# Up projection of a ConvFFN on fp16 halves with one scale for all its weights, measured by squares in the mLSTM

## The chip, the cores and the metric

The kernel runs on one core of one Trainium2 chip. The core has a matrix engine (TensorE, PE in the profile, with its weight loads as PEld), a vector engine (VectorE, DVE), an activation engine (ScalarE, ACT), a general engine (GpSimd, POOL) and a sequencer that issues most DMAs (SyncE, SP). ACT issues DMAs too, in order with its other instructions. The metric is the device time of one execution in microseconds (us), as a median of several.

## The reference

One layer of a diffusion backbone with D = 1024, 1024 latent tokens and 256 context tokens: a modulated RMSNorm, one input projection that feeds a bidirectional mLSTM with 4 heads and a windowed attention with 16, a gated merge with residual, and then a ConvFFN with 2816 hidden units. Cut to what matters here:

```python
def conv_ffn(h, w_up, conv_w, conv_b, w_down):
    L = h.shape[1]
    u = h @ w_up                       # (1024, 1024) @ (1024, 5632)
    r = CONV_W // 2
    up = jnp.pad(u, ((0, 0), (r, r), (0, 0)))
    acc = conv_b
    for j in range(CONV_W):
        acc = acc + up[:, j:j + L] * conv_w[j]
    a, g = jnp.split(acc, 2, axis=-1)
    return (jax.nn.silu(g) * a) @ w_down

x_mid = x + g1[:, None, :] * y         # y: the merged branches, mLSTM and attention
x = x_mid + g2[:, None, :] * conv_ffn(modulate(rms_norm(x_mid, norm2_w[l]), sh2, sc2), ...)
```

Inputs and outputs are fp32.

## The kernel before

The program is one stream of code in stages: modulation and input projections, attention, mLSTM, branch projections and merge, up projection with convolution and gate, down projection. The framework places each instruction in its engine's order by a schedule of its own; each engine then runs its instructions strictly in that order, and waits on semaphores. So a row's place on an engine is not its place in the code.

**Pairs.** Products that need more accuracy than one pass gives are made from a high and a low half of each operand: `split_from` (L50) writes the high half by an ACT copy (`copy_act`, L46, its instruction is L47) and the low half by a DVE subtraction (L54, or L56 with a scale). Three matmuls make one product: high by high, low by high, high by low (`mm3`, L158, L163 to L165 in the trace; `product`, L2011, L2015 to L2017). The input and mLSTM projections use fp16 halves, with scales measured from the weights themselves (`ScaledWeights`, squares on L112). The branch, up and down projections use fp32 halves of a rounded kind (fp32r), where no scale is needed.

**The up projection** (`Units`, L2020) treats w_up in 22 units of 1024 x 256 columns, each read by one 1 MB DMA. A unit is multiplied by a scheme of 7 products instead of 8, with sums of quarters of the weights (`prep`, `prep2`: tiles s, then q1, q2, r1, r2 as pairs) and of the activations (`put`, L1872: b11, b21, b22, t1 to t4 as pairs, made once). Each product has 4 steps of 3 matmuls of 128x128 by 128x512, into PSUM tiles pa, pb, pc. ACT and DVE take these out into ua and ug; `conv_gate` (L2145) makes convolution and gate of them on ACT and DVE (tile cv), and `hidden_sums` makes sums for the down projection. The loop at L2227 runs one unit after another, the splits of the next unit beside the products of this one. The pools op4 (10 tiles of 128x1024 fp32) and op2 (4 of 128x512) hold pair halves.

**The mLSTM** runs head by head (loop L1569). For head h+1 it prepares the two weight groups (`prepare`, squares wjw on L112), splits them (whkv and wlkv for keys and values, whqo and wlqo for queries and the output gate), then multiplies the latent blocks one by one (`proj_kv`, L1308: 8 blocks of 128 tokens, 24 matmuls each; k and VH are ACT copies, VL a DVE split), transposes the keys (`trans_k`, kT to kh and kl), updates states (`states`, dC and C, with CH an ACT copy), and projects the queries (`proj_q`, q to qh and ql). `core` (L1446) multiplies S from queries and keys, masks and decays it (ub), splits it (sh, sl) and makes the outputs (o, i, nm). `proj_o` and the tiles mo and sg are the output gate. In between, `branch_sums` (L1530) loads pieces of the branch weights and of the attention output on ACT's queue (s_ba, t_at, s_bm), forms sums for the branch projections on DVE and stores them; its tile has two buffers, so that a load waits for the store of the second-last set.

Of the kernel before, what the change touches and what calls it, by code (L numbers as in the profile page):

```python
# [171 lines left out]
@with_exitstack  # L172
def layer_kernel(ctx: ExitStack, tc: tile.TileContext, A: dict, out: bass.AP, dbg=None):
    nc = tc.nc
    dbg = dbg or {}

    cp = ctx.enter_context(tc.tile_pool(name="cp", bufs=1, reuse_waits="tile"))
    dr = ctx.enter_context(tc.tile_pool(name="dr", bufs=1, space=DRAM, reuse_waits="tile"))

    ident = cp.tile([P, P], F32, name="ident")  # L180
    nc.sync.dma_start(ident, A["ident"])
    expo = cp.tile([P, 16], F32, name="expo")
    nc.gpsimd.memset(expo, -0.5)
# [71 lines left out]
    if dbg.get("stop") in ("hT", "att"):
        ph1.close()
        psx_t.close()
        psx.close()
        return
    with ExitStack() as st:  # L260
        stage_mlstm(E, st)
    if "mlT" in dbg:
        dump(nc, tc, mlT_d, dbg["mlT"])
    E.gcx.close()
    ph1.close()
    if dbg.get("stop") == "ml":
        psx_t.close()
        psx.close()
        return
    with ExitStack() as st:  # L270
        stage_tail(E, st)
    psx_t.close()
    psx.close()
# [977 lines left out]
def stage_mlstm(E, st):  # L1251
# [56 lines left out]
    def proj_kv(h):  # L1308
        w, f = H[h].pop("wkv"), H[h]["fkv"]
        ks, vs = [None] * NBLK, [None] * NBLK  # L1310
        for j in orders(h)[0][1]:
# [10 lines left out]
            else:  # L1322
# [207 lines left out]
    def branch_sums():  # L1530
# [21 lines left out]
        for j, o in enumerate(res):  # L1552
            nc.sync.dma_start(E.sums_d[n][:, j, i], o)

    rwp = st.enter_context(tc.tile_pool(name="mlr4", bufs=4, reuse_waits="tile"))
    prepare(0)
    bp = st.enter_context(tc.tile_pool(name="mlb", bufs=15, reuse_waits="tile"))
# [3 lines left out]
    proj_q(0)  # L1561
    proj_kv(0)
    E.kvx.close()
    trans_k(0)
    states(0)
    masked(0)
    decays(0, nullcontext())
    for _ in range(2):
        branch_sums()  # L1569
    for h in range(MLH):  # L1570
        core(h)
        proj_o(h)
# [12 lines left out]
        if h + 1 < MLH:  # L1585
            proj_q(h + 1)
            for _ in range((3, 4, 3)[h]):
                branch_sums()


def stage_tail(E, st):
# [46 lines left out]
    def x512(name, dt=F32R, pool=None):  # L1638
# [2 lines left out]
            nx[0] += 1  # L1641
        return xts[pool].tile([P, 512], dt, tag="x", name=name)


    g1b = tp1.tile([P, D], F32, name="g1b")
    g2b = tp1.tile([P, D], F32, name="g2b")
# [174 lines left out]
        nc.sync.dma_start(g1b, E.g_d[0].to_broadcast([P, D]))  # L1821
    branch("m", sgm_d, 6)

    def norm_factors():

        nc.vector.scalar_tensor_tensor(m2[:, 1], m2[:, 1], 1.0, vecT[:, V_N2 : V_N2 + KT], op0=ALU.add, op1=ALU.mult)
        nc.vector.tensor_scalar(m2[:, 1], m2[:, 1], float(D) ** 0.5, None, op0=ALU.mult)

    sM.close()

    accp = sA.enter_context(tc.tile_pool(name="accp", bufs=8, side="right", reuse_waits="tile"))
# [93 lines left out]
    def weight_sums(k, a0, a1, b0, b1, eng=None):  # L1925
# [8 lines left out]

    psc = E.psx_s
    U = Units(
        nc, lambda j: A["w_up"][j], lambda n: rawp.tile([P, KT, 256], F32, tag="raw", name=n), op4, op2,
        lambda tag, n: dict(A=mm_tile, F=E.fl_tile, B=tp_tile, C=lambda n: E.c_tile(n))[tag](n),
        lambda tag, n: accp.tile([P, L], F32, tag="a", name=n), B,
    )  # L1940
# [3 lines left out]
    for i, b in enumerate((4, 5, 6, 7, 0, 1, 2, 3)):  # L1944
# [7 lines left out]
    norm_factors()  # L1952
# [16 lines left out]
    square(5)  # L1969
    scale(4)  # L1970
    U.lead(0)
    U.prep_apart(0, lambda n, dt=F32R: x512(n, dt, 1))
    scale(5)
    first_half(H)
    project(1, 6, w)
# [44 lines left out]
class Units:  # L2020

    def __init__(self, nc, src, raw, op4, op2, bank, out, B):
        self.nc, self.src, self.raw, self.op4, self.op2, self.bank, self.out, self.B = nc, src, raw, op4, op2, bank, out, B
        self.raws, self.R1, self.mid, self.S, self.Q = {}, {}, {}, {}, {}

    @staticmethod
# [5 lines left out]
        return pair[o : o + 4]  # L2034

    def pair(self, j, nm, new, src):
        p = self.v(new(f"{nm}h{j}")), self.v(new(f"{nm}l{j}"))
        split_from(self.nc, *p, src)
        return [(p[0][:, k], p[1][:, k]) for k in range(p[0].shape[1])]

    def lead(self, j):
        self.raws[j] = raw = self.raw(f"ur{j}")
        self.nc.sync.dma_start(raw, self.src(j))
        if j != 2:
            self.R1[j] = self.pair(j, "r1", self.op4, raw[:, :, 0:P])

    def lead_first(self, j):

        raw = self.v(self.op4(f"uf{j}", F32))
        self.nc.sync.dma_start(raw, self.src(j)[:, :, 0:P])  # L2050
        self.R1[j] = self.pair(j, "r1", self.op4, raw)

    def first_mm(self, j):
        nc, B, r1 = self.nc, self.B, self.R1.pop(j)
# [17 lines left out]
    def prep(self, j):  # L2072
# [3 lines left out]
        t(s12[:, 0:4], a21, a22, op=ALU.add)  # L2076
        t(s12[:, 4:8], s12[:, 0:4], a11, op=ALU.subtract)
        self.S[j] = s12
        self.Q[j] = [self.pair(j, "q1", self.op4, s12)]

    def prep2(self, j):
        raw, t = self.raws.pop(j), self.nc.vector.tensor_tensor
# [4 lines left out]
        self.Q[j] += [self.pair(j, "q2", self.op4, s34), self.pair(j, "r2", self.op2, a22)]  # L2087

    def prep_apart(self, j, new):
# [3 lines left out]
        s1, s2, s3, s4 = [self.v(new(f"s{i}_{j}", F32)) for i in range(1, 5)]  # L2093
# [4 lines left out]
        self.Q[j] = [sum([self.pair(j, f"q1{i}", new, s) for i, s in enumerate((s1, s2))], [])]  # L2098
        self.S[j] = s3, s4

    def prep2_apart(self, j):
        h, lo = [self.v(self.op4(f"q2{x}{j}")) for x in "hl"]
        for i, s in enumerate(self.S.pop(j)):
            split_from(self.nc, h[:, 4 * i : 4 * i + 4], lo[:, 4 * i : 4 * i + 4], s)
        r2 = self.pair(j, "r2", self.op2, self.raws.pop(j)[:, 4:8, P:256])
        self.Q[j] += [[(h[:, k], lo[:, k]) for k in range(8)], r2]

    def rest(self, j):
# [328 lines left out]
```

## Time and profile before

| | us |
|---|---|
| median of 3 runs (1849.45 to 1855.98) | 1850.99 |
| the profiled execution | 1858.65 |
| its span in the trace | 1856.9 |
| mean granted clock of TensorE, share of full speed | 0.987 |
| DVE idle until ACT's copy q2h was there (L54), 21 units | 15.8 |
| ACT busy in the window 690 to 975 us (the mLSTM) | 149.44 |

The page gives busy time and its share of the span for each engine, then the chain of work that ended last, and groups of instructions with their mean duration and the idle time ahead of them. A matmul's duration overlaps the next matmul's; the pace of TensorE is read from the distance between two starts. A row of the timeline gives start and duration in us, engine, line, operation, written and read tiles, the form, how many such rows were merged, and in brackets how long the engine idled ahead of it and what ended that.

### The profile page before, as it was taken

Reading aid. Unit: us, or ns where it says so; the run is one execution under the profiler, and the core shown is the slowest. Engines: PE = TensorE matmul, PEld = TensorE weight load, DVE = VectorE, ACT = ScalarE, POOL = GpSimd, SP = SyncE. Lnnn points to the kernel's source line nnn. Section 1 sums busy time; section 2 is a strip of 40 time slices with the busy share of each in tenths; the row PEclk is TensorE's granted clock in tenths of the full one; section 3 lists DMA queues with packets and bytes.
Section 4 is the critical chain, followed back from the end, with each engine's and each line's share of the span. In section 5 each row is a group of like instructions: output and inputs, shape, how many; then the busy total and the mean of one; then the engine's idle time right before and its main releaser. Section 6 shows DMA issues by size and latency. Waiting matters only on the chain.

```text
span 1856.9 us, 27874 instructions
## 1 busy us (share of the span) xinstructions
PE 1795.2 (97%) x9207; PEld 1286.0 (69%) x9207; DVE 1418.6 (76%) x2864; ACT 1070.7 (58%) x2229; POOL 510.5 (27%) x747
## 2 busy tenths in 40 slices
PE   7889999999998899989999999999999999999999
PEld 3855555555555565656668887878888888888887
DVE  3848878888788685858687787698988998896665
ACT  4747777878787564646356563375444444464441
POOL 2467769687762630303020021000000000000000
PEclk9899999999999899999999999999999999999999
DMA  8647988888787724260449936413454544599751
GB/s 336 234 138 147 195 174 177 190 179 196 148 181 138 217 94 161 79 210 32 148 160 359 362 101 221 168 57 125 159 211 180 186 172 154 197 321 369 262 171 68
DMA packets 302193, 342.47 MB, mean 184 GB/s; under 512 B 176208, under 2 KB 200672, under 8 KB 299232
## 3 DMA queue, kind: packets, MB, share of 16 engines
q1 hardware_dynamic: 287648, 314.47, 56.1%
q10 hardware_dynamic: 14400, 26.22, 4.3%
q8 instruction: 72, 1.18, 0.3%
q14 instruction: 73, 0.60, 0.1%
HBM read 224.61 MB, written 76.16 MB: 162 GB/s over the span
## 4 chain that ended last, share of the span: by engine, by line
PE 77%; DVE 7%; DMA 5%; ACT 5%; issue 4%; POOL 3%; ACTq 0%; SPq 0%; POOLq 0%; DVEq 0%
PE g L706 8%; PE pq L706 6%; PE pa L2015 4%; PE pa L2017 4%; PE pa L2016 4%; PE po L706 3%; PE dx L2015 2%; PE dx L2017 2%; PE dx L2016 2%; PE pb L2017 2%; PE pb L2016 2%; PE pb L2015 2%; PE yb L2015 2%; PE yb L2016 2%; PE yb L2017 2%
## 5 line engine op out<-in xcount | busy, mean ns | idle before, releaser
L850 DVE CUSTOM_DVE_ANT_0 s<-s,maskA,nsink 128x640 f32<-128x640 f32 (+1 forms) x128 | 117.5, 918 | 75.0 <-PE s L845 74.6
L866 DVE TENSOR_TENSOR P<-s,P 128x640 f16<-128x640 f32 (+1 forms) x128 | 100.7, 787 | 1.0 <-ACT s L861 1.0
L860 ACT ACTIVATE P<-s,st 128x640 f16<-128x640 f32 (+1 forms) x128 | 98.3, 768 | 4.2
L706 PE MATMUL g<-hH,fh 128*128 128x512 f16 x256 | 97.9, 382 | 0.0
L706 PE MATMUL g<-hH,fl 128*128 128x512 f16 x256 | 97.8, 382 | 0.0
L706 PE MATMUL g<-hL,fh 128*128 128x512 f16 x256 | 97.7, 382 | 0.0
L861 ACT ACTIVATE s<-s,st 128x640 f32<-128x640 f32 (+1 forms) x128 | 93.9, 734 | 0.0
L706 PEld LDWEIGHTS <-hH 128*128 128x128 f16 x640 | 62.1, 98 | 36.5 <-DVE t L770 0.4
L858 ACT ACTIVATE st<-st,shift 128x1 f32<-128x1 f32 x128 | 37.6, 294 | 85.4 <-DVE st L850 84.7
L706 PE MATMUL pq<-wha,hH 128*128 128x384 f16 (+1 forms) x256 | 83.9, 328 | 0.1
L706 PE MATMUL pq<-wha,hL 128*128 128x384 f16 (+1 forms) x256 | 83.9, 328 | 0.0
L706 PE MATMUL pq<-wla,hH 128*128 128x384 f16 (+1 forms) x256 | 83.9, 328 | 0.0
L706 PEld LDWEIGHTS <-fh 128*128 128x128 f16 x512 | 48.1, 99 | 47.9 <-issue 1.6
L2153 ACT ACTIVATE cv<-ua,vecT 128x1024 f32<-128x1024 f32 x22 | 27.4, 1246 | 83.9 <-DVE ua L2126 83.9
L1424 POOL TENSOR_SCALAR kwh<-k,gcall 128x128 fp32r<-128x128 f32 x72 | 33.1, 463 | 154.4 <-PE dC L164 57.1
L163 PE MATMUL kv<-whkv,hH 128*128 128x384 f16 x192 | 63.3, 330 | 6.0 <-DVE VL L56 6.0
L2015 PE MATMUL dx<-dwh,dfh 128*128 128x512 f32 (+1 forms) x176 | 68.3, 388 | 0.0
L2017 PE MATMUL dx<-dwh,dfl 128*128 128x512 f32 (+1 forms) x176 | 68.2, 388 | 0.0
L2016 PE MATMUL dx<-dwl,dfh 128*128 128x512 f32 (+1 forms) x176 | 68.2, 387 | 0.0
L47 ACT ACTIVATE dfh<-drf 128x512 fp32r<-128x512 f32 x55 | 34.3, 628 | 58.5 <-PE dx L2016 26.0
L54 DVE TENSOR_TENSOR dfl<-drf,dfh 128x512 fp32r<-128x512 f32 x55 | 37.7, 691 | 36.5 <-ACT dfh L47 36.4
L164 PE MATMUL kv<-wlkv,hH 128*128 128x384 f16 x192 | 63.2, 329 | 0.4
(691 smaller groups left out, 6253.8 us busy)
## 6 DMA issues: line engine op xcount, KB each, us to landing
ur<-in_w_up SPq DMA_DIRECT2D x22, 1024.0 KB
wmb<-in_w_modB SPq DMA_DIRECT2D x48, 256.0 KB
f_d<-cv SPq DMA_DIRECT2D x22, 512.0 KB
wm<-in_w_modA SPq DMA_DIRECT2D x16, 512.0 KB
fr<-in_w_g SPq DMA_DIRECT2D x32, 256.0 KB
drf<-fs_d SPq DMA_DIRECT2D x15, 512.0 KB
drw<-wt_d SPq DMA_DIRECT2D x14, 512.0 KB
w1b<-in_w_cx SPq DMA_DIRECT2D x16, 388.0 KB
```

Of the source, the lines that this page charges most:

```text
L54: rest = nc.vector.tensor_tensor(lo, src, whole, op=ALU.subtract)
L163: nc.tensor.matmul(ps, lh[:, ls], rh[:, rs], start=start and i == 0, stop=False)
L164: nc.tensor.matmul(ps, lh[:, ls], rl[:, rs], start=False, stop=False)
L706: nc.tensor.matmul(self.ps, x, w, start=self.i == 0, stop=self.i == self.n - 1)
L850: nc.vector.tensor_tensor_reduce(e, e, self.mask, scale=self.ss[:, h : h + 1], scalar=nsink[:, hh : hh + 1], op0=ALU.add, op1=ALU.min, acc ...
L858: nc.scalar.activation(m, st4[:, 8 + h : 9 + h], AF.Identity, bias=shift)
L860: nc.scalar.activation(two[:, :W], e, AF.Exp, bias=m, scale=-1.0)
L861: nc.scalar.activation(e, e, AF.Exp, bias=m, scale=-1.0, accum_out=st4[:, 4 + h : 5 + h])
L866: nc.vector.tensor_tensor(two[:, W : 2 * W], self.e[h], two[:, :W], op=ALU.subtract)
L2015: nc.tensor.matmul(ps, lh, rh, start=start and i == 0, stop=False, skip_group_check=True)
L2016: nc.tensor.matmul(ps, lh, rl, start=False, stop=False, skip_group_check=True)
L2017: nc.tensor.matmul(ps, ll, rh, start=False, stop=stop and i == n - 1, skip_group_check=True)
```

## The change

The up projection's halves become fp16. That needs a scale that brings the weights into fp16's range, one for all of w_up here, in `E.upf[:, 2:3]`. The activations' scale is put into m2, the modulation's factor, and the inverse of both into conv_w, so that the convolution's result stays the same. Both halves of a pair now share one tile of the old size of one half, so that the pools op4, op2 and x512 need half as many slots for pairs.

The scale is measured from the sum of squares of all of w_up: 44 loads of 512 KB on ACT's queue (`up_load`, tile um, a pool of 3 buffers), 44 ACT squares in place with an accumulated sum (`up_square(2)`, after each latent key/value block of heads 1 to 3), and once, in head 3, `up_scales` with one matmul, two small ACT squares, five DVE instructions and ten on POOL. The code of `norm_factors` moves into it. In the trace and in the orders of the changed kernel the lines of the mLSTM lie 5 higher (L1543 for L1538).

```diff
@@ proj_kv
             ks[j] = k
+            if h and j >= NCB:
+                up_square(2)
+            if h == MLH - 1 and vs.count(None) == 1:
+                up_scales()
@@ stage of the mLSTM
+    NUP = 2 * NFC
+    def up_load():
+        n = UP["load"]
+        if n < NUP:
+            raw = UP["raw"][n] = upp.tile([P, 4, 256], F32, tag="up", name=f"um{n}")
+            nc.scalar.dma_start(raw, A["w_up"][n // 2][:, 4 * (n % 2) : 4 * (n % 2) + 4])
+            UP["load"] += 1
+    def up_square(k):
+        for _ in range(k):
+            n = UP["done"]
+            if n < NUP:
+                raw = UP["raw"].pop(n)
+                nc.scalar.activation(raw, raw, AF.Square, accum_out=E.up[:, n : n + 1])
+                UP["done"] += 1
+                up_load()
+    def up_scales():
...
+        nc.tensor.matmul(pb[:, : NUP + 2], E.ones, E.up[:, : NUP + 2], start=True, stop=True)
+        nc.vector.tensor_reduce(f[:, 0:1], pb[:, :NUP], axis=AX.X, op=ALU.add)
...
+        nc.gpsimd.tensor_scalar(f[:, 1:2], f[:, 0:1], 2.0 ** -28, 1e-36, op0=ALU.mult, op1=ALU.add)
+        nc.gpsimd.tensor_tensor(f[:, 2:3], f[:, 1:2], expo[:, 0:1], op=ALU.pow)
...
+        nc.gpsimd.tensor_scalar(m2, m2, f[:, 3:4], None, op0=ALU.mult)
+        cw = vecT[:, V_CW : V_CW + 132]
+        nc.gpsimd.tensor_scalar(cw, cw, f[:, 6:7], None, op0=ALU.mult)
+    upp = ux.enter_context(tc.tile_pool(name="upm", bufs=3, side="right", reuse_waits="tile"))
+    for _ in range(3):
+        up_load()
@@ put
-            B[m][k] = [x512(f"{m}{x}{k}", pool=homes[m]) for x in "hl"]
+            B[m][k] = xpair(f"{m}{k}", homes[m])
@@ Units
     def pair(self, j, nm, new, src):
-        p = self.v(new(f"{nm}h{j}")), self.v(new(f"{nm}l{j}"))
-        split_from(self.nc, *p, src)
+        p = [self.v(t) for t in new(f"{nm}{j}")]
+        split_from(self.nc, *p, src, scale=self.scale)
-        self.Q[j] = [self.pair(j, "q1", self.op4, s12)]
+        self.Q[j] = [self.pair(j, "q1", self.pair4, s12)]
```

The schedule also moves instructions. Three places on ACT matter. The first is the end of head 1's key/value blocks, up to the query copies; whqo are the high halves of the query and gate weights, CH the copies of the state, qh the queries' high half, um the pieces of w_up. Before:

```order
L47 ACTIVATE k_2_8852<-kv_2_8853,wfw_ml_8492 128x128
L47 ACTIVATE VH_2_8879<-kv_2_8853,wfw_ml_8492 128x256
L1546 DMA t_at_0_9051<-attT_d 128x512
L47 ACTIVATE kh_0_8890<-kT_0_8885 128x512
L47 ACTIVATE CH_1_1_8932<-C_1_0_8911 128x258
L47 ACTIVATE kh_1_8899<-kT_1_8894 128x512
L47 ACTIVATE CH_0_1_8945<-C_0_0_8921 128x258
L1546 DMA t_at_0_9051<-attT_d 128x512
L1546 DMA t_at_1_9052<-attT_d 128x512 x2
L47 ACTIVATE qh_0_8990<-q_0_8965,wfw_mlqo_8517 128x512
```

and of the change:

```order
L47 ACTIVATE VH_2_8932<-kv_2_8906,wfw_ml_8503 128x256
L1568 DMA um_8939<-in_w_up 128x1024
L1576 ACTIVATE um_8900,upq<-um_8900 128x1024
L47 ACTIVATE kh_0_8949<-kT_0_8944 128x512
L1568 DMA um_8942<-in_w_up 128x1024
L47 ACTIVATE kh_1_8958<-kT_1_8953 128x512
L47 ACTIVATE CH_1_1_8991<-C_1_0_8970 128x258
L47 ACTIVATE CH_0_1_9004<-C_0_0_8980 128x258
L47 ACTIVATE whqo_0_9008<-wrw_mlqo_0_8511,wfw_mlqo_8528 128x2x384
L47 ACTIVATE whqo_1_9012<-wrw_mlqo_1_8513,wfw_mlqo_8528 128x2x384
L47 ACTIVATE whqo_2_9016<-wrw_mlqo_2_8515,wfw_mlqo_8528 128x2x384
L47 ACTIVATE whqo_3_9020<-wrw_mlqo_3_8517,wfw_mlqo_8528 128x2x384
```

The four whqo splits, which stood ahead of the first key/value block before, now stand behind the last CH, in heads 1 and 2; DVE's wlqo splits follow them there. In head 3 they stay among the blocks.

The second place is ACT at the start of head 2's key/value blocks; wjw are the squares of the next head's weights. Before:

```order
L47 ACTIVATE whqo_3_10159<-wrw_mlqo_3_9704,wfw_mlqo_9715 128x2x384
L47 ACTIVATE k_2_9787<-kv_2_9788,wfw_ml_9690 128x128
L47 ACTIVATE VH_2_9814<-kv_2_9788,wfw_ml_9690 128x256
L1546 DMA t_at_0_10221<-attT_d 128x512 x2
L112 ACTIVATE wjw_ml_0_10894,wqw_ml_10893<-wrw_ml_0_10885 128x768
L47 ACTIVATE k_3_9836<-kv_3_9837,wfw_ml_9690 128x128
L47 ACTIVATE VH_3_9863<-kv_3_9837,wfw_ml_9690 128x256
L1546 DMA t_at_1_10222<-attT_d 128x512 x2
L112 ACTIVATE wjw_ml_1_10896,wqw_ml_10893<-wrw_ml_1_10887 128x768
L112 ACTIVATE wjw_ml_2_10898,wqw_ml_10893<-wrw_ml_2_10889 128x768
```

and of the change:

```order
L1576 ACTIVATE um_9974,upq<-um_9974 128x1024
L1576 ACTIVATE um_9977,upq<-um_9977 128x1024
L1568 DMA um_10016<-in_w_up 128x1024
L47 ACTIVATE k_2_9846<-kv_2_9847,wfw_ml_9749 128x128
L47 ACTIVATE VH_2_9873<-kv_2_9847,wfw_ml_9749 128x256
L1568 DMA um_10068<-in_w_up 128x1024
L1576 ACTIVATE um_10013,upq<-um_10013 128x1024
L47 ACTIVATE k_3_9901<-kv_3_9902,wfw_ml_9749 128x128
L47 ACTIVATE VH_3_9928<-kv_3_9902,wfw_ml_9749 128x256
L1568 DMA um_10071<-in_w_up 128x1024
L1576 ACTIVATE um_10016,upq<-um_10016 128x1024
L1576 ACTIVATE um_10068,upq<-um_10068 128x1024
```

The wjw squares and the branch sums' loads leave the key/value stage for the query stage and `core`, and loads and squares of w_up stand in it.

The third place is ACT between head 3's query copies and its score copies sh. Before:

```order
L47 ACTIVATE qh_0_11400<-q_0_11375,wfw_mlqo_10927 128x512
L47 ACTIVATE qh_1_11429<-q_1_11404,wfw_mlqo_10927 128x512
L47 ACTIVATE sh_1_1_11502<-ub_1_1_10951 128x512
L1475 ACTIVATE nm_1_2_11556<-i_1_2_11552,gcall 128x257
L47 ACTIVATE sh_0_0_11507<-ub_0_0_10954 128x512
```

and of the change:

```order
L47 ACTIVATE qh_0_11557<-q_0_11532,wfw_mlqo_11034 128x512
L1543 DMA s_bm_1_11605<-in_w_bm 128x512
L47 ACTIVATE qh_1_11586<-q_1_11561,wfw_mlqo_11034 128x512
L1543 DMA s_bm_0_11618<-in_w_bm 128x512 x2
L1543 DMA s_bm_1_11619<-in_w_bm 128x512 x2
L47 ACTIVATE sh_1_1_11659<-ub_1_1_11058 128x512
L1480 ACTIVATE nm_1_2_11713<-i_1_2_11709,gcall 128x257
L47 ACTIVATE sh_0_0_11664<-ub_0_0_11061 128x512
```

Four loads of a further branch sum now stand between the query copies and the first score copy.

More of the change, by code (lines that the diff above doesn't have):

```diff
@@ L243, in layer_kernel @@
     E.hs = cp.tile([P, 2], F32, name="hs")
+    E.upf = cp.tile([P, 32], F32, name="upf")
     E.w2 = ScaledWeights(E, tc, ph1)
@@ L1553, in branch_sums @@
             nc.sync.dma_start(E.sums_d[n][:, j, i], o)
+    E.up = mp.tile([P, 64], F32, name="upq")
+    UP = dict(load=0, done=0, raw={})
+    NUP = 2 * NFC
[13 more added lines that the diff above has]
+                up_load()
@@ L1563, in stage_mlstm @@
     E.kvx.close()
+    ux = ExitStack()
+    upp = ux.enter_context(tc.tile_pool(name="upm", bufs=3, side="right", reuse_waits="tile"))
     trans_k(0)
@@ L1588, in stage_mlstm @@
                 branch_sums()
+    ux.close()
 def stage_tail(E, st):
@@ L1642, in x512, with pair16, xpair, pair4 @@
         return xts[pool].tile([P, 512], dt, tag="x", name=name)
+    def pair16(t):
+        n = t.shape[1] // 2
+        return t[:, :n], t[:, n:]
+    def xpair(name, pool):
+        return pair16(xts[pool].tile([P, 1024], F16, tag="x", name=name))
+    def pair4(name):
+        return pair16(op4p.tile([P, 2048], F16, tag="o4", name=name))
+    def pair2(name):
+        return pair16(op2p.tile([P, 1024], F16, tag="o2", name=name))
     g1b = tp1.tile([P, D], F32, name="g1b")
@@ L1936, in stage_tail @@
     U = Units(
-        nc, lambda j: A["w_up"][j], lambda n: rawp.tile([P, KT, 256], F32, tag="raw", name=n), op4, op2,
+        nc, lambda j: A["w_up"][j], lambda n: rawp.tile([P, KT, 256], F32, tag="raw", name=n), op4, pair4, pair2, E.upf[:, 2:3],
         lambda tag, n: dict(A=mm_tile, F=E.fl_tile, B=tp_tile, C=lambda n: E.c_tile(n))[tag](n),
@@ L2020, with __init__ @@
 class Units:
-    def __init__(self, nc, src, raw, op4, op2, bank, out, B):
-        self.nc, self.src, self.raw, self.op4, self.op2, self.bank, self.out, self.B = nc, src, raw, op4, op2, bank, out, B
+    def __init__(self, nc, src, raw, op4, pair4, pair2, scale, bank, out, B):
+        self.nc, self.src, self.raw, self.op4, self.pair4, self.pair2, self.bank, self.out, self.B = nc, src, raw, op4, pair4, pair2, bank, out, B
+        self.scale = scale
         self.raws, self.R1, self.mid, self.S, self.Q = {}, {}, {}, {}, {}
@@ L2044, in lead @@
         if j != 2:
-            self.R1[j] = self.pair(j, "r1", self.op4, raw[:, :, 0:P])
+            self.R1[j] = self.pair(j, "r1", self.pair4, raw[:, :, 0:P])
     def lead_first(self, j):
@@ L2050, in lead_first @@
         self.nc.sync.dma_start(raw, self.src(j)[:, :, 0:P])
-        self.R1[j] = self.pair(j, "r1", self.op4, raw)
+        self.R1[j] = self.pair(j, "r1", self.pair4, raw)
     def first_mm(self, j):
@@ L2086, in prep2, with prep_apart @@
         t(s34[:, 4:8], a12, self.S.pop(j)[:, 4:8], op=ALU.subtract)
-        self.Q[j] += [self.pair(j, "q2", self.op4, s34), self.pair(j, "r2", self.op2, a22)]
-    def prep_apart(self, j, new):
+        self.Q[j] += [self.pair(j, "q2", self.pair4, s34), self.pair(j, "r2", self.pair2, a22)]
+    def prep_apart(self, j, new, new16):
         raw, t = self.raws[j], self.nc.vector.tensor_tensor
         a11, a12, a21, a22 = raw[:, 0:4, 0:P], raw[:, 4:8, 0:P], raw[:, 0:4, P:256], raw[:, 4:8, P:256]
-        s1, s2, s3, s4 = [self.v(new(f"s{i}_{j}", F32)) for i in range(1, 5)]
+        s1, s2, s3, s4 = [self.v(new(f"s{i}_{j}")) for i in range(1, 5)]
         t(s1, a21, a22, op=ALU.add)
@@ L2097, in prep_apart @@
         t(s3, a11, a21, op=ALU.subtract)
-        self.Q[j] = [sum([self.pair(j, f"q1{i}", new, s) for i, s in enumerate((s1, s2))], [])]
+        self.Q[j] = [sum([self.pair(j, f"q1{i}", new16, s) for i, s in enumerate((s1, s2))], [])]
         self.S[j] = s3, s4
     def prep2_apart(self, j):
-        h, lo = [self.v(self.op4(f"q2{x}{j}")) for x in "hl"]
+        h, lo = [self.v(t) for t in self.pair4(f"q2{j}")]
         for i, s in enumerate(self.S.pop(j)):
-            split_from(self.nc, h[:, 4 * i : 4 * i + 4], lo[:, 4 * i : 4 * i + 4], s)
-        r2 = self.pair(j, "r2", self.op2, self.raws.pop(j)[:, 4:8, P:256])
+            split_from(self.nc, h[:, 4 * i : 4 * i + 4], lo[:, 4 * i : 4 * i + 4], s, scale=self.scale)
+        r2 = self.pair(j, "r2", self.pair2, self.raws.pop(j)[:, 4:8, P:256])
         self.Q[j] += [[(h[:, k], lo[:, k]) for k in range(8)], r2]
```

22 lines of the change are left out of this document (17 added, 5 removed).

## The prediction

> **What bounds the kernel now.** I read the busy shares first, then the chain that ended last.
>
> ```profile
> PE 1795.2 (97%) x9207; PEld 1286.0 (69%) x9207; DVE 1418.6 (76%) x2864; ACT 1070.7 (58%) x2229; POOL 510.5 (27%) x747
> PE 77%; DVE 7%; DMA 5%; ACT 5%; issue 4%; POOL 3%; ACTq 0%; SPq 0%; POOLq 0%; DVEq 0%
> ```
>
> TensorE is busy 97% of the span and is 77% of the chain. Those are averages; the change touches two stretches with different limits, the FFN (about 1218 to 1642 us) and the mLSTM (about 690 to 975 us), so I read windows there (columns: length, PE, PEld, DVE, ACT, POOL busy us with counts, PE clock, DMA share, GB/s).
>
> ```profile
> 1300.00:1400.00 100.00, 100.00 (x443) 82.81 (x442) 89.17 (x106) 48.35 (x59) 0.00 (x0) 1.00 0.50 182
> 1225.00:1235.00 10.00, 9.79 (x49) 8.02 (x50) 9.89 (x28) 9.20 (x24) 0.00 (x0) 1.00 0.01 3
> 690.00:975.00 285.00, 270.53 (x1589) 177.05 (x1587) 201.26 (x560) 149.44 (x351) 53.40 (x134) 0.98 0.41 137
> ```
>
> In the FFN's middle PE never rests: a shorter matmul there shortens the kernel, until DVE (89%) takes over. At the FFN's start DVE is already full. In the mLSTM PE rests 14.5 of 285 us and ACT has work for 149; there the change adds work to ACT and the DMA queues.
>
> **What the fp16 operands save.** The row counts 88 `pa<-b11h,r1h` matmuls, 4 for each of 22 units; a unit has 7 products of 4 steps of 3 matmuls, 84, so 1848 matmuls change type.
>
> ```profile
> L2015 PE MATMUL pa<-b11h,r1h 128*128 128x512 f32 x88 | 34.5, 391 | 0.2 <-ACT r1h L47 0.2
> 1219.20 0.39 PE L2017 MATMUL pa<-b11h,r1l 128*128 128x512 f32 x1
> ...
> 1223.96 0.39 PE L2017 MATMUL pc<-b21h,r1l 128*128 128x512 f32 x1
> 953.28 0.38 PE L163 MATMUL mo<-hH,whqo 128*128 128x512 f16 x1
> ...
> 956.30 0.38 PE L165 MATMUL mo<-hH,wlqo 128*128 128x512 f16 x1
> 1400.47 0.69 DVE L2065 TENSOR_TENSOR ua<-pc,ua 128x512 f32<-128x512 f32 x1
> ...
> 1410.32 0.69 DVE L2076 TENSOR_TENSOR s<-ur 128x512 f32<-128x512 f32 x1 [1.30 <-PE pb L2016]
> ...
> 1419.52 0.68 DVE L2065 TENSOR_TENSOR ua<-pc,ua 128x512 f32<-128x512 f32 x1
> ```
>
> "Busy" of a matmul overlaps the next, so I take the spacing of starts. The fp32 pair rows are the first and last of 22: 4.76 us over 21 steps, 226.7 ns. The fp16 rows, of the same 128x512 shape, are the first and last of 15: 3.02 over 14, 215.7 ns. The saving is 11.0 to 11.1 ns; times 1848 it is **20.5 us**. A unit now takes 19.05 us (1400.47 to 1419.52), which is 84 x 226.7; at 215.7 it would take 18.12.
>
> [...]
>
> **What the splits cost DVE.** `split_from` with a scale issues SCALAR_TENSOR_TENSOR (L56) where it issued TENSOR_TENSOR (L54).
>
> ```profile
> L54 DVE TENSOR_TENSOR q2l<-s,q2h 128x1024 fp32r<-128x1024 f32 x21 | 25.7, 1225 | 15.8 <-ACT q2h L47 15.8
> L54 DVE TENSOR_TENSOR r2l<-ur,r2h 128x512 fp32r<-128x512 f32 x22 | 15.1, 688 | 0.0
> L56 DVE SCALAR_TENSOR_TENSOR wlqo<-wrw_mlqo,wfw_mlqo,whqo 128x768 f16<-128x768 f32 x12 | 11.6, 1012 | 0.0
> ```
>
> The plain form costs (1225 - 688) / 512 = 1.05 ns an element, so 957 ns at 768; the scaled form into fp16 takes 1012, 55 more. Four splits a unit: 0.22 us. DVE waits 0.53, 0.20 and 1.30 us in the unit from 1400.47, the last shown above, so it works about 17.0 of 19.05; then 17.2 of 18.12. Slack falls from 2.0 to 0.9 us a unit, still positive, so PE sets the pace. The added cost is 0 while that holds; if the cover is gone DVE's 17.2 plus its in-order waits sets the unit. Either end: 0, or the whole 20.5 eaten (14 us kept, if a third of the slack turns into waits). Where DVE is full, from 1225 to 1257, 4.9% of 32 us, 1.6 us, isn't gained. I take **-18.5**, range -14 to -20.5. The paired tiles, with fewer slots per pool, only let splits run earlier; their work stays the same, and 0 is taken. The down-projection behind it shifts unchanged.
>
> **What the measurement costs the mLSTM.** 44 loads of 512 KB and 44 squares of 128x1024 go onto ACT's instruction stream and queue.
>
> ```profile
> L392 ACT ACTIVATE xj<-x 128x1024 bf16<-128x1024 f32 x5 | 5.2, 1047 | 7.1 <-DMA x<-in_ctx 7.1
> L392 ACT ACTIVATION_READ_ACCUMULATOR xj<-x 128x1 f32 x5 | 0.9, 187 | 0.0
> L1538 ACTq DMA_DIRECT2D s_bm<-in_w_bm x16: 334/360/1337, 822.0 to 911.5; - x16
> ```
>
> A square with its read-out is 1.23 us, 44 are 54 us; 44 issues at 0.35 are 15 us. ACT has 135 us free in the window, so the 70 us fit on average; the price is in order, and the orders shown with the change say where.
>
> The first term is **q's weights**. For heads 1 and 2 the four `whqo` splits move from ahead of the key/value blocks to behind `kh` and `CH`.
>
> ```profile
> 721.30 1.09 PE L1353 MATMUL kT<-ident,k 128*128 128x128 f32 x8
> ...
> 722.48 0.39 PE L163 MATMUL q<-hH,whqo 128*128 128x512 f16 x1
> 723.27 0.42 ACT L47 ACTIVATE CH<-C 128x258 fp32r<-128x258 f32 x1
> L47 ACT ACTIVATE whqo<-wrw_mlqo,wfw_mlqo 128x768 f16<-128x768 f32 x12 | 10.2, 921 | 0.0
> ```
>
> PE began q at 722.48, in head 1. Now the first `whqo` follows the last `CH`: 723.69 + 0.92 = 724.61, 2.1 us late. The third matmul needs `wlqo`, 1.01 us behind it, 0.6 more; one um issue ahead, 0.35: 3.0 us. After such a gap the clock drops:
>
> ```profile
> 704.62 0.32 PE L163 MATMUL kv<-whkv,hH 128*128 128x384 f16 x1 [0.58 <-DVE VL L56]
> ...
> 708.35 0.33 PE L165 MATMUL kv<-whkv,hL 128*128 128x384 f16 x1
> 711.32 0.48 PE L163 MATMUL kv<-whkv,hH 128*128 128x384 f16 x1 [2.64 <-DVE VL L56]
> ...
> 711.92 0.52 PE L165 MATMUL kv<-whkv,hL 128*128 128x384 f16 x1
> 712.24 0.52 PE L163 MATMUL kv<-whkv,hH 128*128 128x384 f16 x1
> ...
> 714.48 0.35 PE L164 MATMUL kv<-wlkv,hH 128*128 128x384 f16 x1
> ...
> 805.23 0.32 PE L163 MATMUL kv<-whkv,hH 128*128 128x384 f16 x1 [2.48 <-DVE VL L56]
> ```
>
> The block from 704.62 to 708.35 runs 23 steps of 0.162 us; after the 2.64 us wait steps are 0.32 until 714.48, about ten, so the wait cost 1.6 us more. With it q's wait is 4.6 us a head, 9.2 for two. It can't be negative, since those splits only move behind work.
>
> [...]
>
> The second term is the **loads ahead of q's splits and of the score copies**.
>
> ```profile
> 822.01 4.53 ACTq L1538 DMA_DIRECT2D s_bm<-in_w_bm  x3
> 826.59 0.69 ACT L47 ACTIVATE qh<-q,wfw_mlqo 128x512 fp32r<-128x512 f32 x1 [5.80 <-DMA s_bm<-in_w_bm]
> 828.11 0.33 PE L163 MATMUL S<-qh,kh 128*128 128x128 f32 x1 [1.65 <-DVE ql L56]
> ...
> 831.99 0.39 PE L163 MATMUL o<-VH,sh 128*128 128x258 f32 x1 [1.54 <-ACT sh L47]
> ...
> 833.66 0.39 PE L165 MATMUL o<-VH,sl 128*128 128x258 f32 x1 [1.05 <-DVE sl L54]
> ```
>
> A branch-sum load waits for its tile's store and ACT stands behind it: PE lost 1.65 + 1.54 + 1.05 = 4.2 us in head 2. Such loads now stand there in all three heads: 2.5 us each in heads 1 and 2, where the later q start hides a part, and 4.2 + 1.6 in head 3: 10.8. Bounds are 0 and 3 x 5.8 = 17.
>
> The third is the **squares among the key/value blocks**.
>
> ```profile
> 700.50 0.84 ACT L112 ACTIVATE wjw_mlqo<-wrw_mlqo 128x768 bf16<-128x768 f32 x1 [2.67 <-DMA wrw_mlqo<-in_w_mlqo]
> ```
>
> This square waited 2.67 us for its load, and PE felt 0.58 of it, at 704.62. About 34 squares, 17 pairs, fall into the three key/value stages. Bounds: 17 x 0, since 11 squares replace 8 shorter ones there; and 17 x 2.67 = 45. If half the pairs wait, at the felt 0.58, it is 5 us; one of the two gaps (2.64, 2.48) may stay, 2.6: together 7.6.
>
> Sum after: 9.2 + 10.8 + 7.6 = 27.6. The waits of before that these replace: 0.58 + 2.64 + 2.48 + 4.2 + 2 x 1.6, and about 0.9 of slow clock behind 833.66: 14. The mLSTM grows by **13.5**. `up_scales` runs among head 3's last blocks, with one matmul; its POOL chain ends long before the FFN: 0.
>
> **Sum.** -18.5 + 13.5 = -5. The profiled execution took 1858.65 us (span 1856.9), so it would take 1853.65. The median shown, 1850.99, lies 7.66 lower; on it the forecast is **1846 us**.
>
> **The rivals.** B: the scheduler hides the squares, since ACT has 135 us free, and the mLSTM grows by 0 to 4: 1830.5 to 1836. For: the wjw squares and sums that crowded the key/value stage are moved out. Against: q's weights stand last in the order. C: squares waiting for DMA hold ACT in front of the key and value copies; it decides from a loss of 28 us, which is 17 pairs at 1.2 us in place of 0.44 with the other terms held. At 17 x 2.67 the mLSTM grows by 45 or so, the net is +26: 1860 to 1877, slower. For: 700.50; against: PE felt a fifth of it. D: DVE sets the FFN's unit, through evacuations that stand behind splits in its order; at 18.8 us a unit the gain is 5, the net +8.5: 1859. For: slack of 0.9. Against: the 1.30 wait goes as splits run earlier. E: the saved spacing is larger, DVE's 17.2 sets the unit: 22 x 1.85 = 41 saved, 13.5 given back: 1824. Against: the fp16 rows hold 215.7 in a row with nothing waiting.
>
> [...]
>
> That it doesn't do what it says (a spacing of 226.7 kept) would leave +13.5, 1864; the fp16 rows speak against it, and I give it nothing of its own.
>
> **Chances.** Forecast 0.45, with the mLSTM at +4 to +20 (1836 to 1853); B 0.22; C 0.23; D 0.08; E 0.02. A measurement of this kernel tells about 0.5%, 9.3 us, from no change: bounds 1841.7 and 1860.3. Faster: 0.15 of the forecast, B, E: 0.39. Same: 0.30 of the forecast, 0.07 of C, 0.05 of D: 0.42. Slower: 0.16 of C and 0.03 of D: 0.19. The range goes from B's foot, 1830.5 (-20.5 with nothing added), into C to 1866, where about one in ten is left out above.
>
> **What would show it.** Up matmuls 215.7 ns apart and units of 18.1 us with PE at 100%: the first term. DVE waits of about 0.9 us a unit left: the second. A PE wait ahead of q in heads 1 and 2, of 2.5 to 3.5 us with slow matmuls behind it; waits ahead of S and o in each head; kv waits of under 3 us. If the mLSTM (prepare of head 1 to the first `yb`) grows by under 4 or over 28 us, the third part is wrong. If units are over 18.4 us, the second is.

## The result and the profile after

The change is slower: 1883.26 us (median of 4) against 1852.75 for the kernel before, ratio 1.0155, 95% interval 1.0133 to 1.0176. The two profiled executions took 1881.69 and 1858.65 us, 23.0 apart; the medians are 30.5 apart, mainly because the profiled execution of before lies above all its timed runs. The traces are compared with each other below.

The busy shares on the page of the change:

```profile
PE 1788.1 (95%) x9209; PEld 1124.5 (60%) x9209; DVE 1429.4 (76%) x2867; ACT 1123.5 (60%) x2321; POOL 519.0 (28%) x758
```

TensorE is busy for less time (1788.1 for 1795.2 us) and rests more. The windows show where. They are cut at the same events in both kernels: first key/value block, first `yb` product, first `pa` product, first `dx` product. Columns as before. Before:

```profile
683.00:967.60 284.60, 269.99 (x1615) 176.59 (x1614) 200.86 (x558) 151.74 (x352) 54.57 (x138) 0.99 0.40 133
967.60:1218.80 251.20, 250.23 (x1105) 204.43 (x1106) 189.84 (x297) 132.13 (x249) 22.33 (x19) 0.99 0.65 236
1218.80:1641.60 422.80, 422.04 (x1865) 347.91 (x1864) 378.57 (x485) 219.29 (x297) 2.47 (x1) 1.00 0.47 170
```

After:

```profile
683.00:995.00 312.00, 280.94 (x1607) 179.44 (x1608) 201.24 (x560) 189.26 (x428) 60.82 (x144) 0.96 0.55 180
995.00:1245.60 250.60, 249.25 (x1104) 204.44 (x1104) 191.60 (x299) 134.30 (x252) 22.31 (x19) 0.99 0.66 239
1245.60:1664.00 418.40, 405.32 (x1866) 182.02 (x1865) 389.65 (x495) 228.07 (x298) 3.01 (x1) 1.00 0.52 180
```

The whole difference lies in two stages. The mLSTM takes 27 us more, the FFN only 4.4 us less. In the mLSTM's row the same matmuls are busy 11 us longer at a lower granted clock (0.96 for 0.99), and the remaining 16 us are waits. (A part of the 11 us is not clock: the last matmul ahead of a wait counts with its whole duration, 0.33 us for a kv matmul where starts are 0.162 us apart, and the profile lists 30 waits of PE ahead of the first `yb` where it listed 12.) In the FFN's row PE's work did fall by 17 us, but 13 us of waits stand where there were 0.8, and DVE is busy 389.65 of 418.4.

The waits of PE in the change's mLSTM, from its timeline (last field: idle before, and who ended it):

```profile
722.12 0.61 PE L163 MATMUL q<-hH,whqo 128*128 128x512 f16 x1 [1.99 <-ACT whqo L47]
...
724.11 0.61 PE L165 MATMUL q<-hH,wlqo 128*128 128x512 f16 x1 [0.53 <-DVE wlqo L56]
...
826.80 0.39 PE L163 MATMUL q<-hH,whqo 128*128 128x512 f16 x1 [0.92 <-ACT whqo L47]
...
829.47 0.61 PE L165 MATMUL q<-hH,wlqo 128*128 128x512 f16 x1 [1.64 <-DVE wlqo L56]
...
859.85 0.38 PE L163 MATMUL i<-CH,qh 128*128 128x258 f32 x1 [2.54 <-DVE nm L1481]
...
871.72 0.39 PE L163 MATMUL i<-CH,qh 128*128 128x258 f32 x1 [2.13 <-DVE nm L1481]
```

The first four are the forecast waits for q's weights, 2.5 us a head. The last two are of a kind that wasn't: inside `core`, ahead of i, where PE lost 0.4 us in all before. PE waited there for DVE's addition `nm`. DVE's timeline shows what stood ahead of it:

```profile
857.57 0.69 DVE L1552 TENSOR_TENSOR t_at<-t_at 128x512 f32<-128x512 f32 x1 [2.51 <-DMA t_at<-attT_d]
...
859.38 0.74 DVE L1481 TENSOR_TENSOR nm<-nm,o 128x257 f32<-128x257 f32 x2
...
870.64 0.69 DVE L1544 TENSOR_TENSOR s_bm<-s_bm,s_bm 128x512 f32<-128x512 f32 x1 [1.83 <-DMA s_bm<-in_w_bm]
871.25 0.42 DVE L1481 TENSOR_TENSOR nm<-nm,o 128x257 f32<-128x257 f32 x1
```

The first instruction of a branch sum waits for its load, and `nm` stands behind it. ACT's timeline shows why the load came late:

```profile
852.52 0.81 ACTq L1551 DMA_DIRECT2D t_at<-attT_d  x2
853.38 0.63 ACT L47 ACTIVATE sh<-ub 128x512 fp32r<-128x512 f32 x1 [2.42 <-DMA t_at_d<-t_at]
...
865.54 2.01 ACTq L1543 DMA_DIRECT2D s_bm<-in_w_bm  x4
867.59 0.73 ACT L47 ACTIVATE CH<-C 128x258 fp32r<-128x258 f32 x2 [5.73 <-issue]
```

Branch-sum loads that wait for a store (`t_at_d<-t_at` in the bracket of the `sh` row) now stand in the middle of `core`. ACT's score and state copies wait behind the loads' issues, and DVE's branch sums wait for the loads: 16.8 us over the mLSTM, 9.2 before. The squares themselves waited for their loads only 3.0 us in four places; the schedule had spread them over all heads, from 653.6 to 914.6 us.

In the FFN the chain goes from DVE to ACT to PE. First the last product into a `pb` tile and what DVE did until it added that tile to `ua`:

```profile
1414.69 0.38 PE L2079 MATMUL pb<-b,q 128*128 128x512 f16 x1
...
1415.92 0.69 DVE L1957 TENSOR_TENSOR wa<-wa 128x512 f32<-128x512 f32 x1 [0.80 <-DMA wa<-in_w_dn]
1416.53 1.28 DVE L56 SCALAR_TENSOR_TENSOR r<-ur,upf,r 128x1024 f16<-128x1024 f32 x1
1417.72 0.68 DVE L2189 TENSOR_TENSOR ua<-pb,ua 128x512 f32<-128x512 f32 x1
```

Then ACT, then PE:

```profile
1418.44 1.24 ACT L2216 ACTIVATE cv<-ua,vecT 128x1024 f32<-128x1024 f32 x1 [4.21 <-DVE ua L2189]
...
1422.98 0.58 ACT L47 ACTIVATE ua<-pa 128x512 f32<-128x512 f32 x1
```

```profile
1422.51 0.38 PE L2078 MATMUL pc<-b,r 128*128 128x512 f16 x1
1422.72 0.38 PE L2079 MATMUL pc<-b,r 128*128 128x512 f16 x1
1423.61 0.38 PE L2077 MATMUL pa<-t,q 128*128 128x512 f16 x1 [0.51 <-ACT ua L47]
```

The matmuls run 0.216 us apart as forecast. But a sum of the down projection's weights, which waited 0.80 us for its load, and a split stood ahead of the addition in DVE's order. So ACT waited 4.21 us for it, the copy that frees `pa` came late, and PE waited for that. In the whole FFN PE waited 7.1 us in 11 places for this copy; before it never did.

### The profile page after: what moved, and what is told of

It reads as the page before. It is cut to its first block, busy times and chain, and to the rows that moved or that the text cites. A ratio compares the mean times of both kernels' runs of the same rounds, so it can differ in the third digit from the quotient of the medians.

```text
span 1879.6 us, 27964 instructions
## 1 busy us (share of the span) xinstructions
PE 1788.1 (95%) x9209; PEld 1124.5 (60%) x9209; DVE 1429.4 (76%) x2867; ACT 1123.5 (60%) x2321; POOL 519.0 (28%) x758
## 4 chain that ended last, share of the span: by engine, by line
PE 60%; DVE 20%; DMA 9%; issue 5%; POOL 3%; ACT 3%; SPq 1%; ACTq 0%; DVEq 0%; POOLq 0%
PE g L707 8%; PE pq L707 6%; PE po L707 3%; PE yb L2079 2%; PE yb L2077 2%; PE yb L2078 2%; PE dx L2077 2%; PE dx L2079 2%; PE dx L2078 2%; DVE cv L2218 2%; DVE cv L2217 2%; PE dy L2078 2%; PE dy L2077 2%; PE dy L2079 2%; DMA fa<-f_d 1%
## 5 line engine op out<-in xcount | busy, mean ns | idle before, releaser
L47 ACT ACTIVATE q<-s,upf 128x1024 f16<-128x1024 f32 (+1 forms) x46 | 50.8, 1110 | 57.3 <-DVE s L2140 33.2
L2077 PE MATMUL pa<-t,q 128*128 128x512 f16 x176 | 66.7, 379 | 7.3 <-ACT ua L47 7.1
L2079 PE MATMUL pa<-t,q 128*128 128x512 f16 x176 | 66.7, 379 | 0.0
```

The source lines that it names most:

```text
L47: return nc.scalar.activation(out, in_, AF.Copy, scale=scale)
L2077: nc.tensor.matmul(ps, lh, rh, start=start and i == 0, stop=False, skip_group_check=True)
L2079: nc.tensor.matmul(ps, ll, rh, start=False, stop=stop and i == n - 1, skip_group_check=True)
```

## The experiments

In the table, mLSTM is the time from the first key/value block to the first `yb`, FFN from the first `pa` to the first `dx`, each from the run's own trace. One trace is one execution: the seven runs that share e1's mLSTM (e1, f1, f2, f3, g1, h1, v1) spread from 279.3 to 286.1 us there, and the eight that share the change's FFN (the change, e1, e3, e4, m1, m2, m3, n1) from 417.5 to 420.7. A difference within these spreads says nothing by itself.

| run | mLSTM us | FFN us | ratio to before, 95% |
|---|---|---|---|
| before | 284.5 | 422.8 | 1 |
| the change | 311.3 | 418.4 | 1.0155 (1.0133 to 1.0176) |
| e1_fixed_scale | 282.6 | 419.4 | 0.9991 (0.9978 to 1.0004) |
| e2_squares_alone | 314.0 | 423.7 | 1.0192 (1.0167 to 1.0217) |
| e3_loads_alone | 290.8 | 417.5 | 1.0030 (1.0015 to 1.0046) |
| e4_squares_no_loads | 289.1 | 420.3 | 1.0039 (1.0027 to 1.0050) |
| m1_q_weights_first | 322.1 | 420.7 | 1.0187 (1.0155 to 1.0219) |
| m2_pinned | 327.6 | 420.7 | 1.0247 (1.0218 to 1.0275) |
| m3_pinned_sp | 314.7 | 419.1 | 1.0179 (1.0162 to 1.0196) |
| n1_loads_on_sp | 289.4 | 419.1 | 1.0042 (1.0031 to 1.0054) |
| f1_sums_on_pool | 285.3 | 452.7 | 1.0169 (1.0146 to 1.0192) |
| f2_plain_splits | 284.2 | 419.4 | 0.9976 (0.9963 to 0.9989) |
| f3_8_4 | 279.3 | 414.7 | 0.9991 (0.9975 to 1.0008) |
| g1_no_sums | 283.8 | 406.9 | 0.9919 (0.9900 to 0.9937) |
| h1_early6 | 286.1 | 419.7 | 1.0052 (1.0037 to 1.0067) |
| v1_plain_8 | 282.0 | 413.3 | 0.9977 (0.9962 to 0.9992) |

### The two halves apart

```diff
 # e1: no loads, no squares
+    nc.gpsimd.memset(E.up, 1.0)
...
-            if h and j >= NCB:
-                up_square(2)
...
-        up_load()
```

> The change without its measurement: no loads of w_up and no squares in the mLSTM, the sums set to a constant that gives the same scale; the fp16 up projection as in the change. If the 26.8 us that the mLSTM grew by (683.5 to 994.8 us in the trace of the change, 683.1 to 967.6 before) all come from loads and squares, the mLSTM is back at 284 to 287 us, the FFN keeps its 418 us (423 before), and the time is 4 to 5 us under the kernel before, ratio 0.997. Rival: the FFN gains little only because something of the measurement reaches into it; then it gains 15 to 18 us here and the ratio is 0.990.

> The kernel before with the 44 loads and 44 squares alone, the up projection on fp32 pairs as it was. If the two halves of the change add up, it is 26 to 28 us slower than before, ratio 1.0145, and slower than the change by 4 to 5 us. Rival: part of the mLSTM's loss is the chain that forms the scales; then it loses under 20 us.

e2 puts `up_load` and `up_square` into the kernel before and nothing else. Without its measurement the change is not clearly faster than before (0.9991, with 1 inside the interval; the forecast ratio of 0.997 was missed). The FFN keeps 419.4 us, so the poor gain is its own. The measurement alone costs the mLSTM 29.5 us and the kernel 37 us by the medians, more than the 26 to 28 expected; with e1's 0.9991 it adds up to the change's ratio within the intervals. The chain that forms the scales is ruled out: e2 doesn't have it.

### Loads or squares

```diff
 # e3: loads without squares
-                nc.scalar.activation(raw, raw, AF.Square, accum_out=E.up[:, n : n + 1])
 # e4: squares of one tile that stays, pinned behind the key copy, no loads
+                with tc.issue_after(kc.ins):
+                    up_square(2)
-                nc.scalar.activation(raw, raw, AF.Square, accum_out=E.up[:, n : n + 1])
+                nc.scalar.activation(us, um, AF.Square, accum_out=E.up[:, n : n + 1])
```

> The change with its loads but without the squares (the sums constant). Theory that the DMA traffic and the loads' places in ACT's queue cost the time: 15 us or more over the run with neither. Theory that ACT's time costs it: within 5 us of the run with neither.

> The change with 44 squares of a tile that stays in SBUF, each pair issued behind its block's key copy, and no loads. In ACT's order whqo then stands ahead of the blocks as before. Theory that ACT's 54 us of squares cost the time: 15 us or more over the run with neither. Theory that the order of the other work (q's weights late, branch sums and wjw squares in core) or the loads cost it: under 8 us over it.

Neither is dear: over e1, the loads cost the mLSTM 8.2 us and the squares 6.5 in these traces (7 and 9 us by the ratios), though ACT is busy 195.96 us in e4's mLSTM (151.74 before). e3 lies between its two theories; e4, by its trace, fits the one that ACT's time isn't the cost. The sum is 15 or 16, not 29. The rest needs both. It isn't the traffic either: the DMA engines' share in e3's mLSTM is 0.57, in the change's 0.55.

### The order, undone in two ways

```diff
 # m1: q's weights split right behind the key/value weights
             load_kv(h + 1)
+            rq, fq = H[h + 1]["w_mlqo"]
+            H[h + 1]["wsplit"] = w2.load(rq, fq, f"qo{h + 1}")
...
 # m2: the change, with the squares pinned
-                up_square(2)
+                with tc.issue_after(kc.ins):
+                    up_square(2)
```

> The change with the splits of q's weights written behind those of the key/value weights, so that ACT's order has whqo ahead of the blocks again; squares, loads and all else as in the change. If the late weights cost what the trace shows (waits of 1.99 + 0.53 and 0.92 + 1.64 us ahead of q, and 1 to 3 us of slow clock), it is 5 to 9 us faster than the change, and 20 us of the mLSTM's loss stay. Rival, that they are the root of the other waits in core too: 15 us or more faster.

> The change with each pair of squares issued behind its block's key copy, as written, loads included. The order of wjw squares, branch sums and q's weights is then near that of before. Theory that the moved order costs the time: the mLSTM (kv to yb) takes 288 to 296 us against 311 in the change, 15 us or more faster than the change. Rival, that squares behind their loads hold up the key copies: 303 us or more, under 8 us faster.

m1 met neither of its expectations, and m2 met the rival's. With q's weights early the waits for them are gone, and others (up to 4.1 us, ahead of o in head 3) took their place: the mLSTM got 11 us longer in the trace, while the intervals of the two ratios overlap. With the squares pinned it is 327.6 us. ACT's timeline of m2, first blocks of head 1:

```profile
698.30 0.20 ACT L1577 ACTIVATION_READ_ACCUMULATOR um<-um 128x1 f32 x1
703.01 1.06 ACT L1577 ACTIVATE um<-um 128x1024 f32<-128x1024 f32 x1 [4.51 <-DMA um<-in_w_up]
...
704.58 0.37 ACT L47 ACTIVATE k<-kv,wfw_ml 128x128 f32<-128x128 f32 x1 [0.41 <-ACT um L1577]
```

A square waits 4.51 us for its load and the key copy waits behind it. In all, squares waited 21.7 us in 16 places. e4 has the squares pinned in the same way without this wait, and is 38.5 us shorter in the mLSTM.

### The queue

```diff
 # n1: the change; m3: m2
-            nc.scalar.dma_start(raw, A["w_up"][n // 2][:, 4 * (n % 2) : 4 * (n % 2) + 4])
+            nc.sync.dma_start(raw, A["w_up"][n // 2][:, 4 * (n % 2) : 4 * (n % 2) + 4])
```

> The change with its 44 loads on SyncE's queue instead of ACT's. Theory that the issues on ACT (44 of 0.34 us, and what stands behind them) are a main part of the mLSTM's 27 us: 8 us or more faster than the change. Theory that it is the squares waiting for their loads and the work that the schedule pushes into core: within 5 us of the change or slower.

> The change with each pair of squares pinned behind its block's key copy and with the loads on SyncE's queue. Pinned with loads on ACT was 1.0247 of the kernel before (mLSTM 327.6 us, squares waiting 21.7 us for loads). Theory that the loads' place in ACT's order is what costs: 1.003 to 1.006, mLSTM under 295 us, as with squares of a resident tile. Theory that squares in the key/value stage wait for loads through three buffers whichever queue issues them: 1.015 or more, mLSTM over 305 us and waits for um of 10 us or more.

n1 takes 22 of the 27 us back, as its first theory has it. But it doesn't try the issues alone, since the schedule then places the squares elsewhere. The two lines of the loads and squares, as a group by tile, are telling (shortest, median and longest in ns, then first and last start in us; the last line gives us and times waited); first n1, then m3:

```profile
L1568 SPq DMA_DIRECT2D um<-in_w_up x44: 327/328/772, 627.6 to 769.7; - x44
L1576 ACT ACTIVATE um<-um x44: 1039/1050/1061, 645.1 to 779.1; 128x1024 f32<-128x1024 f32 x44
```

```profile
L1569 SPq DMA_DIRECT2D um<-in_w_up x44: 327/328/1335, 627.6 to 921.2; - x44
L1577 ACT ACTIVATE um<-um x44: 1041/1056/1058, 688.9 to 925.6; 128x1024 f32<-128x1024 f32 x44
...
  DMA um<-in_w_up: 25.7, 21
```

In n1 the squares are over at 779, in head 1's `core`, and PE's waits in heads 2 and 3 are much like those of before: up to 2.64 us ahead of kv, and 1.58, 1.34 and 1.05 ahead of S and o (1.65, 1.54 and 1.05 before). Its squares waited 11.4 us in 7 places, and one of these is behind PE's longest wait:

```profile
733.56 1.06 ACT L1576 ACTIVATE um<-um 128x1024 f32<-128x1024 f32 x1 [5.12 <-DMA um<-in_w_up]
734.52 0.19 ACT L1576 ACTIVATION_READ_ACCUMULATOR um<-um 128x1 f32 x1
734.61 0.67 ACT L47 ACTIVATE qh<-q,wfw_mlqo 128x512 fp32r<-128x512 f32 x1
...
736.12 0.48 PE L163 MATMUL S<-qh,kh 128*128 128x128 f32 x1 [5.05 <-DVE ql L56]
```

In m3, on the same queue but pinned, squares waited 25.7 us in 21 places, and the mLSTM takes 314.7 us, as its second theory has it. Pinned, the queue was worth 13 us (m2 to m3) of the 45 that m2 lies over e1. So the loads' place in ACT's queue is a part of the cost. The rest is a square that waits for its load where PE soon needs ACT; that more than three buffers would bring the loads in time was not tried. In the change the schedule avoids that wait and pays with the order of `core` instead. How its 27 us divide between single displaced instructions isn't settled: m1 shows that one put back moves the wait.

### DVE in the FFN

f1, g1, f2 and f3 are e1 with one edit; h1 and v1 are f2 with one edit more. f1 and g1 take the down projection's sums, of its weights and of the hidden rows, off DVE: f1 moves them to POOL, g1 leaves them out. f2 has no scale on the weights, so conv_w takes out the activations' scale alone. v1 is f2 with f3's 8 slots.

```diff
 # f1: the hidden rows' sums; the weights' sums likewise
+        pt = nc.gpsimd.tensor_tensor
-        tt(o[:, t0], fa[:, t0], fa[:, t1], op=ALU.subtract)
+        pt(o[:, t0], fa[:, t0], fa[:, t1], op=ALU.subtract)
...
 # f2
-        split_from(self.nc, *p, src, scale=self.scale)
+        split_from(self.nc, *p, src)
 # f3
-    ... left("ffo", 10) ...
+    ... left("ffo", 8) ...
 # h1: f2, and
-    E.w_early = 3
+    E.w_early = 6
```

> The change without its measurement, and with the sums of the down projection's weights and of the hidden rows (4 of 128x512 a unit, 0.68 us each on DVE) on POOL. Theory that DVE sets the FFN's pace after the change: from 419 us (pa to dx) it falls to 403 to 409, 10 to 16 us faster than the run with the sums on DVE. Rival, that PE's waits come from the order on ACT and DVE and not from how much DVE does: 415 us or more.

> The change without its measurement, and without the sums on DVE that the FFN makes for the down projection (8 units' weight sums and 11 units' hidden sums, 4 subtractions each, some 50 us of DVE in 420); their loads and stores stay. Theory that DVE's load sets the FFN's pace after the change: pa to dx falls from 419 us to 401 to 406, where TensorE at 215.7 ns is full. Rival, that PE's waits come from the order on ACT and DVE whatever the load: 414 or more.

> The change without its measurement and without the scale on the weights: their splits are plain subtractions again, into fp16, 55 to 60 ns shorter each; conv_w takes out the activations' scale alone. Theory that DVE's time sets the FFN's pace: 0.22 us a unit, 4 to 5 us faster than with the scale. Rival, the order: within 2 us.

> The change without its measurement, with 8 slots instead of 10 in the pool of the pairs, so that splits run less far ahead of their products. Theory that the run-ahead fills DVE's order with work that isn't due: 4 us or more faster than with 10. Theory that DVE's load alone counts: within 2 us, or slower.

> The kernel with fp16 halves and no scale on the weights (no measurement, plain splits; the run of that kind was 0.9976 of the kernel before), and with six instead of three units' weight sums made ahead of the FFN, where DVE has room. By DVE's load: 12 subtractions, 8 us of DVE less in the FFN, 4 to 8 us faster than that run, ratio 0.993 to 0.996. Rival, that the sums only move the wait to the projections ahead: ratio 0.997 or more.

> fp16 halves with no scale on the weights and no measurement (0.9976 of the kernel before when run alone), with 8 slots instead of 10 for the pairs (0.9991 with the scale, FFN 415 us in its trace against 419). By DVE's load nothing more comes: 0.996 to 0.999. If the shorter run-ahead is worth the 4 us of that trace: 0.994 to 0.996.

g1 shows where the FFN's waits come from. With e1's FFN first, then g1's:

```profile
1212.70:1632.10 419.40, 405.70 (x1866) 182.14 (x1865) 389.57 (x495) 228.10 (x298) 3.01 (x1) 1.00 0.51 180
```

```profile
1214.10:1621.00 406.90, 402.53 (x1865) 182.22 (x1865) 349.68 (x429) 229.45 (x299) 3.01 (x1) 1.00 0.52 186
```

With 40 us less on DVE, PE's idle time falls from 13.7 to 4.4 us, and the wait that the change's rows named is all but gone (us in total, times, longest):

```profile
PE pa L2071 <- ACT ua L47: 7.8, 14, 1.7
```

```profile
PE pa L2072 <- ACT ua L47: 0.6, 2, 0.3
```

406.9 us is just outside the 401 to 406 of the theory of DVE's load. And g1 doesn't tell load from place: the 66 instructions that it leaves out are the ones that stood ahead of late additions, some of them waiting for loads of their own (3.7 us in e1). The smaller edits speak against load alone. f2 and h1 leave DVE 384.68 and 377.68 us, 5 and 12 less than e1, and PE's idle time stays (14.8 and 14.4); f3 leaves DVE its load (389.77), and PE's idle time falls to 9.9. Which instructions cost how much isn't settled.

f1 was meant to show the same as g1 and went the other way. Its split of q on DVE took 1618 ns in the mean:

```profile
L56 DVE SCALAR_TENSOR_TENSOR q<-s,upf,q 128x1024 f16<-128x1024 f32 x41 | 66.3, 1618 | 10.2 <-ACT q L47 10.1
```

In the change it is 1281. Of the 42 splits of this form in f1's FFN, the 15 that overlap a POOL instruction took 2.2 us in the mean, the other 27 1.28. DVE's 66 instructions less made it busier, 407.77 us, and the FFN 33 us longer: it is no test of the load.

f2's shorter splits left the FFN's trace at 419.4; its 0.24% is clear of zero, but not shown to come from there. f3 and v1 have an FFN 5 to 6 us shorter in their traces, outside the spread of the others, but the stage ahead of it is 2 and 4 us longer (252.5 for e1's 250.4, 253.1 for f2's 248.9). f3's interval includes no change, and v1's ratio is f2's, so the shorter run-ahead isn't shown to gain anything. Sums made earlier (h1) made that stage, 969.0 to 1231.3, 13 us longer (262.3 for f2's 248.9), and the FFN no shorter, as its rival has it. The best versions, f2 and v1, beat the kernel before by 0.2%. They do without the measurement and the scale, which these weights, drawn with a spread of 1/32, allow; weights far from fp16's range were not tried.

## Why the prediction was wrong

**The matmul.** Right: 0.216 us apart. PE's busy time in the FFN fell by 16.7 us, and by 19.5 in g1, where few waits are left, for the 20.5 counted.

**"Slack falls from 2.0 to 0.9 us a unit, still positive, so PE sets the pace."** This step failed. A unit took 19.1 us (21 steps of the addition `ua<-pc`, 1252.7 to 1653.3), over the 18.4 that the prediction names as the sign of it. The splits cost what was counted: 42 of q 59 ns more each, 42 of r 53 to 56, some 5 us. DVE's load in the FFN's window grew by 11.1 us (378.57 to 389.65), but the rest of that is work of the down projection that now comes before the first `dx`; behind it DVE has 7.0 us less (136.63 for 143.61). What failed is the mean: a slack of 5% a unit didn't cover single additions that came late in DVE's order (2.7 us after the product's end in the rows above), with ACT and then PE behind them. The term -18.5 measured -4.4. (Of its own making it had 0.4 too little: 20.5 less 1.6 is 18.9.) This is rival D, priced at a gain of 5 and given a chance of 0.08.

**q's weights.** The wait of 3.0 us a head measured 2.5 and 2.6. But its price wasn't that of the edit: with it gone (m1), nothing was won.

**The mLSTM's sum.** The mLSTM grew by 26.8 us, twice the 13.5. Taken apart, the forecast has 12.9 us more of waits and 0.7 of slow clock (three times 1.6, less the 4.1 of before). Measured were some 16 of waits, and matmuls busy some 11 longer at the lower clock (0.96 for 0.99). Not every wait of 2 to 2.6 us was followed by a lower clock: it was 0.50 behind the 2.64 us of before (711.3 to 714.5) and behind the change's 1.99 ahead of q (722.1 to 728.7), but 1.00 behind the 2.48 of before (805.2 to 808.0), where the forecast has 1.6, and behind the change's 2.54 ahead of i (859.8 to 862.0). So the term that was mis-sized most is the slow clock, counted behind three waits only (a part of the 11 us is the whole durations of matmuls ahead of more waits). The waits were near in size, and partly by luck: those ahead of q, S, o and kv came to 16.0 us for the 22.8 counted, while those ahead of i and of the state products dC, 9.8 us, stood at nothing. The prediction priced branch-sum loads ahead of the query and score copies, but not further into `core`, where DVE's branch sums wait for them too. The squares' waits for their loads, 5 us of PE's time in the sum, were 3.0 us on ACT.

**Rival C** had the sign and nearly the size (28 us as its point of decision), but another place: squares holding the key copies. That is what m2 and m3 show when they are pinned there, and not what the change shows. Its sums are off as well: with the other terms held, 17 pairs at 1.2 us make a loss of 26, and at 2.67 one of 51, not 45.

**The sum.** -5 us was forecast between the profiled executions; they lie 23.0 apart. Both terms erred to the same side.

## What to carry to other kernels

A shorter matmul is worth its saving only as far as the next engine has slack where the products need it: here a mean slack of 5% behind a chain through two in-order engines left 4 of 20 us. Work added to a free engine is cheap or dear by what stands behind it: 44 squares cost the mLSTM 6.5 us with their data at hand (e4), and with their loads from 7 (n1, early and from another queue) to 45 (m2), behind loads that came late or in an order bent around them. Before building a cheaper path that needs a measurement, run it once with the measurement's result given: here that showed no gain to pay with.

## What the runs showed of the hardware

With 128x512 fp32 subtractions on POOL, some of DVE's instructions in f1 were longer than in the change: the scaled split of 1024 elements 1618 ns for 1281, the longest of the four convolution taps of 1023 elements 2035 for 1277 in the mean, another 1274 for 1276, while POOL itself took 1.3 to 2.1 us for one. Where a split overlapped a POOL instruction it took 2.2 us, elsewhere 1.28.

Stages with more waits had a lower granted clock: 0.93 over m1's mLSTM, with 25 waits of up to 4.1 us and matmuls busy 285.93 us, against 0.99 and 269.99 in the kernel before, with 12 waits of up to 2.64. That the waits bring the clock down was not tried by itself, and it doesn't follow their number alone: m2, with 34, had 0.95.
